# Five load semaphores instead of eight in a row-maximum kernel that streams its input

## The chip, the cores and the metric

One core of one Trainium2 chip. The metric is the device time of one execution in microseconds (us), median of several runs, lower is better. "Span" is the length of the profiled execution on the core; the timed number is some 1.8 us longer.

## The reference

```python
# x: 8192 x 8192 float32, standard normal
def reference(x):
    return np.linalg.norm(x, ord=np.inf, axis=1)   # the largest |x| of each row
```

Each element is read once, and almost nothing is written: 268.4 MB in, 32 KB out.

## The kernel before

A partition gets 64 rows: 47 "head" rows, in loads of two rows (one load has one row), and 17 "tail" rows, in 28 loads that shrink from 16384 columns to 704. SyncE issues all 52 loads, VectorE takes the maximum of the absolute values of each, GpSimd joins the parts of tail rows that were cut. Loads go to a ring of three places of 16384 columns. Load i counts on semaphore i modulo `SEMS`, and since a semaphore may count one load at a time, load i is issued only after the reduction of load i - `SEMS`. The ring adds a wait of its own: the reduction that last read the place must be done.

```python
P = 128
R = 2
RING = 3 * 16384
APART = 2048
SEMS = 8
# ... (sizes of the tail's loads)

class Pieces:
    def __init__(self, tc, ring):
        self.tc, self.nc, self.ring, self.head = tc, tc.nc, ring, 0
        self.sems = [tc.alloc_semaphore(f"loaded{i}") for i in range(SEMS)]
        # ...
    def load(self, at, w, src):
        i = self.started
        self.started += 1
        ins = self.nc.sync.dma_start(out=self.ring[:, at : at + w], in_=src)
        ins.then_inc(self.sems[i % SEMS], 16)
        # ...
        if i >= SEMS:
            self.tc.add_manual_dep(
                ins.ins,
                self.last[i - SEMS].name,
                # ...
                reason="the semaphore counts one load at a time",
            )
    def reduce(self, pairs):
        i = self.reduced
        self.reduced += 1
        for k, (dst, src) in enumerate(pairs):
            ins = self.nc.vector.tensor_reduce(
                out=dst, in_=src,
                axis=mybir.AxisListType.X, op=mybir.AluOpType.max,
                apply_absolute_value=True,
            )
            if k:
                self.tc.keep_in_program_order(ins)
            else:
                ins.wait_op(self.sems[i % SEMS], 16 * (i // SEMS + 1), "sem-ge")
            # ...
        self.last.append(ins.ins)
        return ins

# the head
    while row < head:
        n = (head - row) % R or R
        at = pieces.room(n * n_cols)
        pieces.load(at, n * n_cols, x_head[:, row * n_cols : (row + n) * n_cols])
        buf = ring[:, at : at + n * n_cols]
        pieces.reduce([(res_head[:, row : row + n], buf.rearrange("p (r m) -> p r m", r=n))])
        row += n
# ... (the tail, joining of parts, three stores)
```

## Time and profile before

| | before |
|---|---|
| time, median of 3 runs | 628.93 us (628.88 to 629.33) |
| span | 627.3 us |
| VectorE busy | 552.2 us, 88% |
| read from memory | 268.44 MB, 428 GB/s over the span |
| VectorE's wait for loads in the head | 70.5 us, 2.1 us a load once under way |
| last load issued, landed | 615.13, 624.0 |

To read it: the loads are one stream that SyncE keeps fed, so its end is set by bytes and rate as long as the queue of issued loads never runs dry. What can be lost is the *lead* of a load: the time from its issue to the landing of the load before it, which is how long the queue still has work. The prediction shows the lines.

### The profile page before, as it was taken

The page shows a single profiled execution, that of the slowest core. Times are in us where ns is not written, and L with a number is a line of the kernel's source. Part 1 is how long each engine was busy: PE and PEld are TensorE (multiplying, and loading weights), DVE is VectorE, ACT ScalarE, POOL GpSimd, SP SyncE. Part 2 cuts the span into 40 slices and gives each one's busy share as a digit, 9 for nine tenths or more (in the row PEclk, how much of TensorE's full clock was granted, in tenths as well). Part 3 has the DMA queues.
Part 4 walks back from the last instruction along what each step waited for, and adds up shares of the span by engine and source line. Part 5 has one row for each costly group of instructions (what it writes and reads, how often), then busy time and mean ns, then how long its engine had stood idle before and what let it go on. Part 6 is the DMA issues. An engine that isn't in the chain of part 4 may idle for free.

```text
span 627.3 us, 175 instructions
## 1 busy us (share of the span) xinstructions
DVE 552.2 (88%) x62; POOL 3.2 (1%) x14
## 2 busy tenths in 40 slices
DVE  1398888988889888898888998888988999999998
POOL 0000000000000000000000000000000000000000
DMA  9999999999999999999999999999999999999997
GB/s 401 401 468 401 468 401 468 401 468 401 468 401 468 401 468 401 460 410 451 418 443 426 443 426 439 430 422 447 405 464 406 454 410 442 430 422 429 425 423 306
DMA packets 7921, 268.48 MB, mean 428 GB/s; under 512 B 1264, under 2 KB 1264, under 8 KB 2416
## 3 DMA queue, kind: packets, MB, share of 16 engines
q1 hardware_dynamic: 7632, 268.44, 99.3%
q10 hardware_dynamic: 288, 0.03, 0.0%
q14 instruction: 1, 0.01, 0.0%
HBM read 268.44 MB, written 0.03 MB: 428 GB/s over the span
## 4 chain that ended last, share of the span: by engine, by line
DMA 58%; DVE 41%; issue 0%; DVEq 0%; SPq 0%
DMA ring<-in_x_dram 58%; DVE res_head L110 22%; DVE parts L110 12%; DVE res_tail L110 5%; DVE ring L110 1%; DVEq L269 0%; SPq L92 0%; DVE idle L222 0%
## 5 line engine op out<-in xcount | busy, mean ns | idle before, releaser
L110 DVE TENSOR_REDUCE res_head<-ring 128x2 f32<-128x16384 f32 (+1 forms) x24 | 404.8, 16865 | 70.5 <-DMA ring<-in_x_dram 70.5
L110 DVE TENSOR_REDUCE parts<-ring 128x1 f32<-128x3136 f32 (+18 forms) x22 | 78.5, 3633 | 0.1
L110 DVE TENSOR_REDUCE res_tail<-ring 128x1 f32<-128x8192 f32 (+1 forms) x8 | 61.2, 7703 | 2.1 <-DMA ring<-in_x_dram 2.1
L110 DVE TENSOR_REDUCE ring<-ring 128x1 f32<-128x1536 f32 (+4 forms) x6 | 8.2, 1443 | 0.0
L211 POOL TENSOR_SCALAR res_tail<-parts 128x1 f32<-128x1 f32 x9 | 2.7, 296 | 615.7 <-DVE parts L110 615.7
L211 POOL TENSOR_SCALAR parts<-parts 128x1 f32<-128x1 f32 x1 | 0.4, 354 | 5.6 <-DVE parts L110 5.6
L258 POOL MEMSET const-bfloat16-1.0<- 128x1 bf16 x1 | 0.1, 101 | 0.0
L258 POOL MEMSET const-uint8-127<- 128x1 uint8 x1 | 0.1, 101 | 0.0
L258 POOL MEMSET const-float32-0.0<- 128x1 f32 x1 | 0.1, 98 | 0.2 <-issue 0.2
L258 POOL MEMSET const-float32-1.0<- 128x1 f32 x1 | 0.1, 98 | 0.0
L222 DVE MEMSET idle<- 1x1 f32 x2 | 0.1, 59 | 0.0
## 6 DMA issues: line engine op xcount, KB each, us to landing
ring<-in_x_dram SPq DMA_DIRECT2D x3, 4096.0 KB, 39.7
ring<-in_x_dram SPq DMA_DIRECT2D x1, 6720.0 KB, 31.1
ring<-in_x_dram SPq DMA_DIRECT2D x1, 5568.0 KB, 34.6
ring<-in_x_dram SPq DMA_DIRECT2D x1, 4544.0 KB, 25.9
ring<-in_x_dram SPq DMA_DIRECT2D x1, 4224.0 KB, 29.5
ring<-in_x_dram SPq DMA_DIRECT2D x1, 4032.0 KB, 26.9
ring<-in_x_dram SPq DMA_DIRECT2D x1, 3584.0 KB, 35.1
ring<-in_x_dram SPq DMA_DIRECT2D x2, 1568.0 KB, 39.0
```

Of the source, the lines that this page charges most:

```text
L110: ins = self.nc.vector.tensor_reduce(out=dst, in_=src, axis=mybir.AxisListType.X, op=mybir.AluOpType.max, apply_absolute_value=True,)
L211: combined = nc.gpsimd.tensor_scalar(out=to, in0=best, scalar1=two[0], scalar2=two[1] if len(two) == 2 else None, op0=mybir.AluOpType.max, ...
L222: tc.keep_in_program_order(nc.vector.memset(idle[:, i : i + 1], 0.0))
L258: nc = _bacc.Bacc("TRN2", target_bir_lowering=False, num_devices=1)
```

## The change

Its intent is to use fewer semaphores, on the view that three spare ones do no work.

```diff
@@ -9,7 +9,7 @@
 R = 2
 RING = 3 * 16384
 APART = 2048
-SEMS = 8
+SEMS = 5
```

The one constant does two things: it sets how many semaphores there are, and how many loads may stand between issue and reduced.

## The prediction

> **What bounds the kernel now.** I read the page first, then the chain of waits in order of time, then the table of windows for the end, then the groups by form, the timeline of the last 70 us and the issues of transfers.
>
> The page, for the whole run:
>
> ```profile
> span 627.3 us, 175 instructions
> DVE 552.2 (88%) x62; POOL 3.2 (1%) x14
> DMA  9999999999999999999999999999999999999997
> HBM read 268.44 MB, written 0.03 MB: 428 GB/s over the span
> DMA 58%; DVE 41%; issue 0%; DVEq 0%; SPq 0%
> L110 DVE TENSOR_REDUCE res_head<-ring 128x2 f32<-128x16384 f32 (+1 forms) x24 | 404.8, 16865 | 70.5 <-DMA ring<-in_x_dram 70.5
> ```
>
> The input is 268.44 MB and it arrives at 428 GB/s over the span, with the transfer engines busy in every slice but the last. VectorE works 88% of the time and its only idle time to speak of, 70.5 us, is spent waiting for a load. The stream of loads is the bound. The table of windows says how it ends (columns: stretch, its length, VectorE busy, GpSimd busy, clock, share of the DMA engines, GB/s):
>
> ```profile
> 52.00:477.00 425.00, 378.47 (x22) 0.00 (x0) 1.00 1.00 433
> 545.00:600.00 55.00, 55.00 (x14) 1.67 (x6) 1.00 0.99 424
> 610.00:615.00 5.00, 5.00 (x3) 0.35 (x1) 1.00 1.01 419
> 620.00:624.00 4.00, 4.00 (x4) 0.00 (x0) 1.00 0.83 324
> ```
>
> In the head (47 rows a partition, loads of two rows) the loads set the pace at 433 GB/s and VectorE waits 2.1 us for each. In the tail (17 rows, 28 loads that shrink from 16384 to 704 columns) both are full: the loads are cut so that each lands just as VectorE has finished the one before. So there is no slack behind a late load in the tail: a landing that slips by 1 us moves the end by about 1 us. What has slack is the queue of loads ahead of VectorE. That is what the change touches, so I looked at who holds back the issuing of loads:
>
> ```profile
> SPq L92 <- DVE res_head L110: 465.4, 24, 27.5
> SPq L92 <- DVE parts L110: 90.9, 16, 20.0
> SPq L92 <- DVE res_tail L110: 40.0, 4, 13.9
> ```
>
> SyncE, which issues all loads, waits for a reduction before 44 of the 52. In the head this is for a place in the ring. In the tail the issues and the reductions stand like this (timeline, merged from several short windows; then the issues with KB and us to landing):
>
> ```profile
> 605.10 0.33 SPq L92 DMA_DIRECT2D ring<-in_x_dram  x1
> 613.07 0.33 SPq L92 DMA_DIRECT2D ring<-in_x_dram  x1
> 615.13 0.33 SPq L92 DMA_DIRECT2D ring<-in_x_dram  x1
> 618.35 2.80 DVE L110 TENSOR_REDUCE ring<-ring 128x1 f32<-128x1344 f32 x2
> 622.20 1.07 DVE L110 TENSOR_REDUCE ring<-ring 128x1 f32<-128x896 f32 x1
> ```
>
> ```profile
> ring<-in_x_dram SPq DMA_DIRECT2D x1, 384.0 KB, 10.1
> ring<-in_x_dram SPq DMA_DIRECT2D x1, 352.0 KB, 8.9
> ```
>
> The last load (352 KB) is issued at 615.13, at once after the 1920-column reduction that is eight loads before it, and lands 8.9 us later, at 624.0; VectorE reduces it from 624.05. The load before it lands at 613.07 + 10.1 = 623.2. So the last load spends nearly all of its 8.9 us standing in the queue behind others; its own bytes take the 0.8 us between these two landings.
>
> **What the Trainium skill says.** "DMA: Bandwidth & Descriptors", section "Why a DMA increments its semaphore by 16 and not by 1", asks for one semaphore for each load in flight, since two loads on one count can pass the wait early. The kernel keeps to that: load i waits until the reduction of load i - SEMS is done. So the number of semaphores is the number of loads that may stand between issue and reduced. The same page, section "Anatomy of one DMA", says that the wait is on the issuing sequencer and that the transfer engines only consume their queues; the trace agrees: the 44 waits before loads are SyncE's, and the DMA share stays near 1.0 through them. It gives about 2 us as the fixed part of a transfer, for another issuing path. Here the first load, into an empty queue, is issued at 0.72 and its reduction starts at 12.93: 12.2 us for 4.19 MB, which at 433 GB/s are 9.7 us. The fixed part is thus about 2.5 us in this trace, and I use that. "Latency and other measured facts" on that page has about 0.6 us to the first byte; here the DMA share is 0 up to 1.5 us and not up to 2.0, so 0.8 to 1.3 us after the issue.
>
> **The change part by part.** Nothing is added to the work: the same 52 loads of the same sizes at the same places, the same reductions, the same stores. Three semaphores go. The only thing that moves is when SyncE may issue a load: after the reduction of load i - 5 rather than i - 8, or after the last reader of its place in the ring, whichever is later.
>
> Head, loads 0 to 23: the ring has three places of two rows, so load i waits for reduction i - 3. Both 5 and 8 are weaker than that. Change: 0.
>
> Early tail, loads 24 to 33: working through the places that the code hands out, each overlaps a load at most five before it, so the ring still decides. Change: 0.
>
> Loads 34 to 51: here the ring would let nearly all of them go six or more loads behind, so with 8 semaphores the count decides from load 39 on, and with 5 from load 34 on. I put the issue right after the end of reduction i - 5 in the trace of before and compare with the landing of load i - 1, that is, how long the queue still has work. Load 37 moves most, from 546.9 to 572.5, and still has 16.8 us of queued work ahead of it. The lead shrinks with the loads: about 9 us at load 42, 5.2 at load 47, 4.6 at 48, 4.2 at 49, 3.7 at 50. For load 51 the releasing reduction is the 1344-column one: 618.35 + 1.54 (by form) = 619.89, so it issues at 619.9 rather than 615.1; the queue has work until 623.2, a lead of 3.2 to 3.3 us.
>
> A load is late only if the lead is shorter than the fixed 2.5 us. Load 51 from an empty queue would land at 619.93 + 2.5 + 0.83 = 623.3, but its turn in the queue comes at 624.0 anyway: 0.7 us to spare. Load 50: issued 618.5, 618.5 + 2.5 + 0.98 = 621.9 against 623.2: 1.2 us to spare. Load 49: 616.8 + 2.5 + 1.06 = 620.4 against 622.1: 1.8 us. All earlier ones have more. So every later issue is hidden, and the sum is 0 + 0 + 0 = 0 us. Three semaphores less may save some hundredths of a microsecond in setting up and clearing; no line of the page shows that cost, and I count 0.
>
> **The rivals.** First, *the queue runs dry at the end*: the 2.5 us was measured on a quiet chip start with one load of 4 MB, and a load issued into a busy queue might need more. At 4 us, load 51 would be late by 0.8 us and load 50 by 0.3; at 5 us the last four loads would be late by at most 1.8 us. These add up little, since a late reduction delays only the load five further on. Time 629.7 to 631. For it: the lead of 3.2 us is of the same size as the fixed part. Against it: what is needed early is the start of the transfer, 0.8 to 1.3 us after the issue, and the completion count overlaps with the next load.
>
> Second, *a shallower queue moves fewer bytes a second*: the sixteen engines of a load finish about 0.4 us apart in the trace, so an engine that runs ahead could be without work if only three loads stand behind the one being reduced. If loads 34 to 51 (some 46 us of transfer, 578 to 624) lost 1%, that is 0.5 us; 3% would be 1.4 us. Against it: at a lead of 3.2 us or more a spread of 0.4 us doesn't empty any queue, and the slowest engine sets the landing.
>
> Third, *a gain*: fewer queued loads disturb each other less, or the end of the program clears fewer semaphores. "Runtime: NRT & Kernel Launch", section on the launch sequence, has the reset of a fixed number of semaphores for each engine, so a smaller count would not shorten it; no run here shows it. The queue is served in order and the head, with only three loads at most outstanding, runs at 433 GB/s against 424 in the middle of the tail with more outstanding. But the tail's loads are smaller, which explains that by itself: each load costs a fixed bit more. At most -0.5 us, 628.4.
>
> **Range and chances.** The centre is the time before with no change, 628.93; I say 629.0, since the only sizeable risks lie above. Three runs of before spread over 0.45 us. The low end is that spread with a small gain, 628.4; the high end is the first rival at its mild form, one microsecond, 630.0. To leave the band of 2% the kernel would have to gain or lose 12.6 us. Nothing found can gain that, and a loss would need some 0.7 us at each of the 18 loads concerned. Chances: 0.01 faster, 0.98 same, 0.01 slower.
>
> **What would show each step right or wrong.** In the changed kernel the head must be the same to the hundredth (VectorE waiting 2.1 us for each load). SyncE's last load should be issued at about 619.9, with the time to landing of the 352 KB load down from 8.9 to about 4.1 us, the 384 KB load's from 10.1 to about 4.7, and landings at the same moments; VectorE should have no new idle time after 520 us, and the DMA share from 600 to 620 should stay at about 1.0. The first rival shows as idle time of VectorE before the 768- and 704-column pieces; the second as a lower rate from 578 us on and landings that slip gradually from load 34; the third as an earlier last landing or a shorter end after the last store. I would be wrong altogether if the head's loads came to wait for the count and not the ring.

## The result, and the profile after

| | before | after |
|---|---|---|
| time, median of 6 runs each | 628.99 us (628.88 to 629.33) | 628.97 us (628.86 to 629.36) |
| ratio | | 1.0, interval 0.9987 to 1.0012 |
| span | 627.3 us | 627.3 us |

The ratios and their 95% intervals come from runs of both kernels in the same rounds, so a ratio is not quite that of the medians. The page of the changed kernel:

```profile
span 627.3 us, 175 instructions
DVE 552.2 (88%) x62; POOL 3.2 (1%) x14
L110 DVE TENSOR_REDUCE res_head<-ring 128x2 f32<-128x16384 f32 (+1 forms) x24 | 404.8, 16865 | 70.5 <-DMA ring<-in_x_dram 70.5
```

The same span, the same instructions, the same 70.5 us of waiting in the head. What SyncE waited for, in the changed kernel (total us, times, longest):

```profile
SPq L92 <- DVE res_head L110: 465.3, 24, 27.5
SPq L92 <- DVE parts L110: 92.0, 16, 20.0
SPq L92 <- DVE res_tail L110: 40.0, 4, 13.9
SPq L92 <- DVE ring L110: 3.8, 3, 1.3
```

The first three are as before. The fourth is new: the last three loads now wait for reductions that write their parts into the ring, the ones five back. SyncE waits longer for its turn there, and no other engine pays for it. The timeline of the changed kernel (start, length), then its issues with KB and us to landing:

```profile
572.42 0.33 SPq L92 DMA_DIRECT2D ring<-in_x_dram  x1
619.90 0.33 SPq L92 DMA_DIRECT2D ring<-in_x_dram  x1
624.03 0.88 DVE L110 TENSOR_REDUCE res_tail<-ring 128x1 f32<-128x710 f32 x1
```

```profile
ring<-in_x_dram SPq DMA_DIRECT2D x1, 384.0 KB, 4.7
ring<-in_x_dram SPq DMA_DIRECT2D x1, 352.0 KB, 4.1
```

The last load is issued at 619.90, which is 4.8 us later than before (615.13), and is reduced from 624.03, where before it was 624.05. Its time to landing falls from 8.9 to 4.1 us: it only stands in the queue for a shorter time. Load 37, issued at 572.42 rather than 546.9, was moved most and also landed where it did before. The table of windows of the changed kernel (columns as in the prediction) for head and tail:

```profile
52.00:477.00 425.00, 378.48 (x22) 0.00 (x0) 1.00 1.00 433
520.00:624.00 104.00, 104.00 (x30) 2.38 (x8) 1.00 1.00 423
```

The rates are those of before (433 and, in the second window, also 423 GB/s), and VectorE has no idle time in the tail's last 104 us.

### The profile page after: what moved, and what is told of

It reads as the page before. It is cut to its first block, busy times and chain, and to the rows that moved or that the text cites. A ratio compares the mean times of both kernels' runs of the same rounds, so it can differ in the third digit from the quotient of the medians.

```text
span 627.3 us, 175 instructions
## 1 busy us (share of the span) xinstructions
DVE 552.2 (88%) x62; POOL 3.2 (1%) x14
## 4 chain that ended last, share of the span: by engine, by line
DMA 58%; DVE 41%; issue 0%; DVEq 0%; SPq 0%
DMA ring<-in_x_dram 58%; DVE res_head L110 22%; DVE parts L110 12%; DVE res_tail L110 5%; DVE ring L110 1%; DVEq L269 0%; SPq L92 0%; DVE idle L222 0%
## 5 line engine op out<-in xcount | busy, mean ns | idle before, releaser
L110 DVE TENSOR_REDUCE res_head<-ring 128x2 f32<-128x16384 f32 (+1 forms) x24 | 404.8, 16865 | 70.5 <-DMA ring<-in_x_dram 70.5
```

Of the source, the lines that this page charges most:

```text
L110: ins = self.nc.vector.tensor_reduce(out=dst, in_=src, axis=mybir.AxisListType.X, op=mybir.AluOpType.max, apply_absolute_value=True,)
```

## The experiments

The theory of the prediction (called A below): a load is late only if its lead is shorter than a fixed part of about 2.5 us, and with five semaphores the shortest lead is 3.2 us. Rivals: B, only the 1 us from issue to first packet counts; C, a loaded queue needs 4 us; D, a shallower queue lowers the rate. If A is right, fewer semaphores must begin to cost at a known point. Four kernels were written for that. Each edit is against the changed kernel.

### Four and three semaphores

```diff
-SEMS = 5
+SEMS = 4      # and, in a second kernel, 3
```

> Four semaphores, nothing else changed. Theory A (the five semaphores are free because a load needs about 2.5 us of queue ahead of it, the fixed part measured on the first load, and with five it has 3.2 us or more): the lead of the last load falls to about 1.95 us, below 2.5, so the end slips by 0.5 us, no load before load 49 is late; time about 629.5. Theory B (only about 1 us, issue to first packet, has to be covered): no change, 0.0 us. Theory C (a loaded queue needs some 4 us): 2.7 us longer, 631.7. Theory D (fewer loads in flight lower the rate of transfers): loads 32 to 45 already land later, with leads of 4 us and more.

> Three semaphores. A (2.5 us needed): head unchanged, since its ring has three places anyway; from about load 43 on the leads fall under 2.5 us, and lateness begins to feed itself, since a late reduction delays the issue three loads on: 3.5 us longer in all, about 632.4; 2.0 us needed would give 2.0 us, 3.0 us would give 5.0. B (1 us): 0.1 us. C (4 us): 9.3 us. D: landings slip in loads 27 to 38 already, where the leads are still 4 to 11 us.

Measured: with four 629.79 us against 628.84 (ratio 1.0015, interval 1.0002 to 1.0027); with three 634.71 against 628.84 (1.0093, 1.0079 to 1.0107). The timeline of the kernel with four:

```profile
624.00 0.95 DVE L110 TENSOR_REDUCE parts<-ring 128x1 f32<-128x768 f32 x1 [0.80 <-DMA ring<-in_x_dram]
624.92 0.89 DVE L110 TENSOR_REDUCE res_tail<-ring 128x1 f32<-128x710 f32 x1
```

VectorE's waits for loads in the tail, in the kernel with three (total us, times, longest):

```profile
DVE res_tail L110 <- DMA ring<-in_x_dram: 3.1, 2, 2.1
DVE parts L110 <- DMA ring<-in_x_dram: 2.0, 3, 0.9
DVE ring L110 <- DMA ring<-in_x_dram: 1.8, 3, 0.8
```

With four, one new gap of 0.8 us stands before load 50, whose lead was 2.2 us; load 49 with 2.6 us and all before it were in time. With three, VectorE waits in the tail at seven more places (2.1 us of the first line was there before), from load 42 on, where the lead is 2.8 us. Loads 27 to 41, with leads of 3.1 us and more, land at their usual intervals. So short leads begin to cost near the 2.5 us that A said; B (no change with four) falls, and D in its general form falls, since a halved queue with leads over 3 us moved the tail's bytes just as fast. But both losses are larger than A's (0.95 instead of 0.5, 5.9 instead of 3.5 us; C's 2.7 and 9.3 are too large), and one fixed threshold doesn't fit: with three, load 42 was 0.6 us late with a lead of 2.8 us, and load 43 another 0.9 us with 3.1 us, where loads 40 and 41 with the same 3.1 us had been in time.

### The last load alone

One load with a short lead, and none after it that could suffer.

```diff
-        if i >= SEMS:
+        back = 3 if i == 51 else SEMS      # and, in a second kernel, 4
+        if i >= back:
             self.tc.add_manual_dep(
                 ins.ins,
-                self.last[i - SEMS].name,
+                self.last[i - back].name,
```

> Five semaphores, but the last load alone waits for the reduction three before it, not five: issued at about 622.3 and not 619.9, so with a lead of 0.8 us. Nothing can feed back, as no load follows. A (2.5 us): lands at 622.3 + 2.5 + 0.83 = 625.6 rather than 624.0, 1.6 us longer. B (1 us): 0.1 us longer. C (4 us): 3.1 us longer. All other loads land as with five.

> Five semaphores, the last load alone waits for the reduction four before it: issued at about 621.2, lead about 1.95 us (0.78 us and 1.54 us late in last_three). A (F = 2.4): 621.2 + 2.4 + 0.83 = 624.4, 0.4 us late. N: its engines run dry about 1 to 1.4 us after the issue, so some start late: 1 to 2 us late, as much as or more than in last_three, though it is issued 1.1 us earlier.

(Theory N in the second text was formed between the two, from the next run but one.) Measured: waiting for the reduction three back 630.38 against 628.84 us (1.0024, interval 1.001 to 1.0038), four back 629.14 against 628.85 (1.0004, 0.999 to 1.0017). Timeline and issue of the kernel with three back:

```profile
622.28 0.33 SPq L92 DMA_DIRECT2D ring<-in_x_dram  x1
625.53 0.89 DVE L111 TENSOR_REDUCE res_tail<-ring 128x1 f32<-128x710 f32 x1 [1.42 <-DMA ring<-in_x_dram]
```

```profile
ring<-in_x_dram SPq DMA_DIRECT2D x1, 352.0 KB, 3.2
```

Its lead was 0.8 us, and 3.2 us from issue to landing less 0.83 us for its 352 KB at 433 GB/s leave a fixed part of 2.4 us. That is A's term, now measured where it is used, and the 1.5 us that it cost is A's 1.6. With four back (lead 1.9 us) the load took 3.0 us, so a fixed part of at most 2.2 us. In the trace it landed at 624.05, 0.1 us later than with five; the 0.3 us between the medians lie within the interval. That is a miss for N, which said 1 to 2, and less than A's 0.4: the fixed part is not quite the same for every load.

### Two semaphores, and the head alone

> Two semaphores: only one load can stand behind the one being reduced, in the head too. A (2.5 us needed): in the head the lead is about 2.1 us, so each two loads slip by about 0.4 us, some 5 us over 24 loads; in the tail each load waits out most of its fixed part: in all about 47 us longer, 676 (36 at 2.0 us, 59 at 3.0). B (1 us): 23 us longer and the head unchanged. C (4 us): 83 us longer. So this run measures the fixed part: the head's landings say it without the tail.

Edit: `SEMS = 2`. Measured: 696.64 us against 628.84 (1.1081, 1.1063 to 1.1099), so 68 us where A said 47 and C 83. The head, which A had slip 5 us, slipped 21 (its last load landed at 479.43 and not at 458.07), and 24 with the load after it. Some of its loads landed in A's time after their issue, others 2 us and more later: for load 3 the trace has all sixteen completion counts within 0.5 us, for load 5 eight of them in a group and eight some 1 to 2 us behind. So it is single transfer engines that come late. Theory N was put up for that: an engine that runs dry *shortly after* a new load is issued may start it later than one that was dry already. If so, issuing a load later can make it land no later. Three kernels test this, with the head alone at two back and the tail as with five. In the second and third, a small extra reduction delays each issue, and fits in VectorE's idle time (the declaration of its target `spare` is left out here).

```diff
+        back = 2 if i < 24 else SEMS
# in the delayed kernels also (448, and 960):
-        pieces.reduce([(res_head[:, row : row + n], buf.rearrange("p (r m) -> p r m", r=n))])
+        pieces.reduce([(res_head[:, row : row + n], buf.rearrange("p (r m) -> p r m", r=n)), (spare, buf[:, :960])])
```

> Five semaphores, but in the head (loads 0 to 23) each load waits for the reduction two before it; the tail is as with five. Each load then has a lead of about 2.1 us. Theory A (a load needs a fixed part F, 2.2 to 2.5 us, whatever the state of the queue): slip of (F - 2.07)/2 for each of 22 loads, 2 to 5 us in all: 631 to 634. Theory N (formed after the run with two semaphores: an engine whose queue runs dry about 1.0 to 1.5 us after the issue starts the new load only some 3 to 3.5 us after the issue, later than an engine that was dry before): about 24 us, as the head of that run had: about 653.

> As head_two, with a reduction of 448 columns into a spare column after each reduction of the head, which the load two further on waits for as well: each issue comes 0.5 us later, lead about 1.6 us. The result is unchanged, the extra reductions fit in VectorE's idle time. A: later is worse, (F + 0.5 - 2.07)/2 a load: 7 to 10 us over the time before, 636 to 639, about 5 us slower than head_two. N: less harm than head_two or about the same, 636 to 653, since the engines now run dry 0.5 to 1.0 us after the issue; which of the two is not known beforehand.

> As head_two_late_half, with 960 columns: issues 1.06 us later, lead about 1.0 us. A: (F + 1.06 - 2.07)/2 a load: 13 to 16 us over the time before, 642 to 645, some 11 us slower than head_two. N: the engines are dry by the time that the new load reaches them, so all start cleanly about 1 us after the issue: the same 13 to 16 us over the time before, but that is about 10 us FASTER than head_two, although every load is issued 1 us later.

| kernel | lead in the head, at first | time | runs from to | ratio to before (interval) |
|---|---|---|---|---|
| head_two | 2.1 us | 652.38 us | 651.27 to 654.26 | 1.0368 (1.0352 to 1.0384) |
| head_two_late_half | 1.5 us | 655.27 us | 653.35 to 657.97 | 1.0423 (1.0399 to 1.0447) |
| head_two_late | 1.0 us | 644.95 us | 644.49 to 645.11 | 1.0255 (1.0239 to 1.027) |

Loads 5 and 7 in the chain of waits of head_two, the kernel that isn't delayed (issue, length of the stretch from issue to landing):

```profile
88.45 23.87 DMA ring<-in_x_dram
129.59 21.76 DMA ring<-in_x_dram
```

and the same two loads in head_two_late, delayed by 1.06 us:

```profile
90.87 21.72 DMA ring<-in_x_dram
130.92 21.83 DMA ring<-in_x_dram
```

Load 5 was issued at 88.45 in one and at 90.87 in the other, and landed at 112.32 and 112.59: an issue 2.4 us later cost 0.3 us. In the delayed kernel loads take 2.2 to 2.6 us beyond their own 19.4 us at nearly every step, which is A's fixed part, and the total of 16 us is at the upper edge of what A and N both gave for it. In the undelayed one they take from 2.4 to 5.8 us; for every second load part of that is the wait behind a late one. So A fails on head_two (631 to 634 expected, 652 measured), and N's surprising claim, that all loads issued 1 us later would make the kernel faster, holds: 7.4 us faster, where N had said about 10. The half delay was no remedy: its 655 us lie above both ranges, A's 636 to 639 and N's 636 to 653.

The DMA packets of load 5 in the two traces show N's step itself. In head_two the engines ended the load before between 1.3 and 1.7 us after the issue of load 5. Six packets then followed without a gap; the first packets of the other ten engines started only 2.7 to 3.2 us after the issue, and took 2.6 to 3.3 us where the usual packet takes 2.4. In head_two_late the engines were dry 0.2 to 0.7 us after the issue, and all sixteen started 1.0 to 1.7 us after it, with first packets as slow. (They run dry some 0.4 us before the count that the lead is measured to.) The lead by itself doesn't decide, though: in the delayed kernel every second load had a lead of 2.4 us and none was late, and last_four had escaped at 1.9.

### How much lead is enough

To issue earlier than in head_two, each head reduction was cut in two, and the load two further on waits for the first part alone; its place in the ring was free a reduction earlier. The second part goes to a spare column, so the result is wrong for some rows (with 256 and 512 columns the comparison with the reference passed all the same, with 1536 it did not).

```diff
+        back = 2 if i < 24 else SEMS
-        self.last.append(ins.ins)
+        self.last.append(first if i < 24 else ins.ins)      # first: the first part
-        pieces.reduce([(res_head[:, row : row + n], buf.rearrange("p (r m) -> p r m", r=n))])
+        rows = buf.rearrange("p (r m) -> p r m", r=n)
+        cut = n_cols - 256      # 512, 1536
+        pieces.reduce([(res_head[:, row : row + n], rows[:, :, :cut]), (spare[:, :n], rows[:, :, cut:])])
```

> As head_two, but each head reduction is cut in two: first all but 256 columns of each row, then these 256 into a spare column; the load two further on waits for the first part alone (its place in the ring was free one reduction before). The result leaves out the maxima of those columns on purpose and is wrong for some rows. Issues come about 0.6 us earlier than in head_two, lead about 2.6 to 2.7 us. A (F = 2.4): no slip, the time before. N (an engine that runs dry somewhat after a new load was issued restarts late): the engines now run dry 1.6 to 2.0 us after the issue; if the new descriptors are safely there by then, the time before; if the danger reaches so far, up to 24 us longer. So this and the next run show how much lead is enough.

> As head_two_early with 512 columns in the second part: issues about 1.15 us earlier than in head_two, lead about 3.2 us, the lead that the last load has with five semaphores. A: the time before. N: at this lead the last load of the changed kernel was in time, so the time before or within 2 us of it; a slip of several us would say that the changed kernel's last loads are near the edge.

> As head_two_early with 1536 columns in the second part: the lead in the head is about 5.3 us. At leads of 2.6 and 3.2 us the stream still lost 15.6 and 13.6 us, with single transfer engines up to 2.5 us behind the others, and an engine that leads the last one by 2.5 us has that much less queue. If that is the cause, 5.3 us are enough even for the engine furthest ahead (5.3 - 2.5 = 2.8 against 1 us from issue to first packet, or 2.5 to landing): the time before within 1 us. If merely having one load queued behind another costs something, whatever the lead, it stays about 10 us longer. The result leaves out maxima on purpose, as in head_two_early.

| kernel | lead in the head, at first | time | runs from to | ratio to before (interval) |
|---|---|---|---|---|
| head_two_early | 2.6 us | 644.61 us | 642.44 to 647.33 | 1.0249 (1.0213 to 1.0285) |
| head_two_earlier | 3.2 us | 642.62 us | 639.11 to 645.14 | 1.0229 (1.0202 to 1.0256) |
| head_two_5us | 5.3 us | 629.57 us | 629.48 to 629.85 | 1.0011 (0.9994 to 1.0027) |

The windows of head_two, then of the kernel with 5.3 us, from 52 to 452 us (the last column is the rate):

```profile
52.00:452.00 400.00, 337.69 (x20) 0.00 (x0) 1.00 0.97 409
```

```profile
52.00:452.00 400.00, 358.56 (x41) 0.00 (x0) 1.00 1.00 433
```

A's "the time before" fails at 2.6 and 3.2 us. In both traces the first loads at two back are in time or nearly so, their sixteen counts within 0.7 us; then at load 6 single engines are late, the counts of one load spread to 2.4 us and stay spread by 1 to 3.4 us. With such a spread the engine that is ahead has that much less queue than the lead says, so it can run dry next; this last step is argued, not shown. At 5.3 us the rate is the full 433 GB/s, and only load 23, the last of the head, was 1 us late. The trace puts this 1 us in the middle of that load, on one engine, and so not down to the lead: a packet at 443.25, after a gap of 0.3 us, took 3.08 us instead of 2.42, just after an 8 KB packet of the instruction queue at 442.93. In the changed kernel this instruction packet comes at 624.5, after the last load. All five kernels with extra reductions have it in the head (442.9 to 472.4), with a slow packet of a load (2.95 to 3.08 us) 0.3 us behind it. So the added instructions probably have a cost of their own, of up to 1 us; no run separates it. The rest agrees with the expectation of a 2.5 us spread on top of 2.5 us, and speaks against a cost of merely having one load queued behind another.

### Count or depth

```diff
-SEMS = 5
+SEMS = 40
+DEPTH = 5
-        if i >= SEMS:
+        if i >= DEPTH:
-                self.last[i - SEMS].name,
+                self.last[i - DEPTH].name,
```

> Forty semaphores, of which no load shares one with any of the 39 before it, and still at most five loads between issue and reduced. If only the depth counts (the theory): the same as with five, issue of the last load at about 619.9, within 0.1 us of the time before. If the number of semaphores costs something in setting up, clearing or waiting (a rival of the prediction): 32 more than before, so any cost of some hundredths each would show as 1 us or more; the three fewer of the change would then have gained a tenth of that and hidden a loss of the same size.

Measured: 629.26 us against 628.92 (1.0006, 0.9992 to 1.002). The last load was issued at 619.86 and landed within 0.03 us of the kernel with five, so the depth alone sets when loads go. The five runs (629.10 to 629.48) nevertheless lie just above the nine of before (628.74 to 629.09). One place is seen: the instruction that clears semaphores at the end of the program took 0.29 us with forty, 0.11 with eight and 0.09 with five. That is 0.2 us of the 0.3; where the rest goes is open. Three fewer save 0.02 us, far below the spread.

## Why the prediction was right

*The head does not change.* Right: 70.5 us of waiting and 433 GB/s in both, since the ring, three places deep, is the stronger wait.

*The ring decides up to load 33, the count from 34 on.* Right: load 33 was issued at its old time, load 34 was the first to move (by 8.5 us), load 37 moved most.

*The last load is issued at 619.9, takes 4.1 us, lands when it did; the 384 KB load takes 4.7.* Right to 0.1 us, and so was "no new idle time", with a DMA share of 1.01 from 600 to 620 us.

*The fixed part of 2.5 us.* Right in size for a load that finds the queue all but dry: 2.4 us (last_three), at most 2.2 (last_four), 2.2 to 2.6 (head_two_late).

*"0.7 us to spare" and "a load is late only if the lead is shorter than the fixed 2.5 us".* This step carried the right conclusion, but it is not a safe margin, and that it held for the last loads is in part luck: with three semaphores load 43 was late with a lead of 3.1 us. In the head with two loads outstanding, leads of 2.6 and 3.2 us were not enough, since single engines came late by up to 2.5 us. In this the prediction's first rival ("a load issued into a busy queue might need more", 4 us) was nearer, and so was the second (an engine that runs ahead is left without work), which the prediction dismissed since the spread was 0.4 us: the spread stays at 0.4 us only as long as no engine has been late. That five semaphores are free rests on what was measured, six runs within 0.5 us and every load in time in the one that was traced, and not on the 0.7 us.

*Fewer semaphores to clear count 0.* 0.02 us in the trace. The remark that the count would not matter at the end was wrong for the kernel's own clearing, at that size.

Slips in the working, none of which changes a conclusion: 618.5 + 2.5 + 0.98 is 622.0 and not 621.9, and 384 KB take 0.91 us at 433 GB/s and not 0.98; with five semaphores four loads, not three, stand behind the one being reduced; the transfers of loads 34 to 51 run from 571.5, so they are 52.5 us and not 46. That a small load costs "a fixed bit more" is so in the trace of before: load 47 landed 1.43 us after load 46, and its 576 KB at 433 GB/s are 1.36 us.

Open: what makes one of sixteen engines start a queued load up to 2 us late, and why a lead of 2.4 us is enough in one kernel and 3.2 us not in another. The traces show the engine's gap and a slow first packet, and not the reason. Nor do the runs say how often the changed kernel's last loads, with leads of 3.2 to 4.3 us, would be hit over many more executions.

## What to carry to other kernels

A limit on the number of loads in flight costs nothing while the queue's lead, the time from a load's issue to the landing of the load before it, stays long; so work the lead out for every load, above all where loads get small, and compare it with issue-to-landing less the load's own bytes. Do not take the time that a lone load needs (2.4 us here) as the limit: in a running stream of 8 MB loads 3.2 us were too little and 5.3 us enough. And test a depth a step or two below the one that you want to ship: five cost nothing here, four 0.95 us, three 5.9, two 68.

## What the Trainium skill lacked or had wrong

- "DMA: Bandwidth & Descriptors", sections on queues and on the anatomy of one DMA: nothing on transfer engines that come late to a load which was queued before they ran dry. Here single engines lost up to 2 us or more each time, which took the head from 433 to 409 GB/s at a lead of 2.1 us, and issuing 1.06 us later made the kernel 7.4 us faster. Nor does that page have how much lead a stream needs: between 3.2 and 5.3 us in this head.
- The same page gives the fixed part as about 2.0 us, fitted on the path through GpSimd. On SyncE's path it was 2.4 us with the queue all but dry (3.2 us for 352 KB, last_three).
- The same page has about 0.6 us to the first byte on SyncE's path and doesn't say from when. Here it holds from the end of the issue: the first packet of the program started 0.63 us after that, and 1.0 us after the issue's start; in last_three and head_two_late engines that were dry before started 0.95 us after the start at the earliest.
- "Runtime: NRT & Kernel Launch", launch sequence: it has the reset around the kernel and not the clearing inside it, which grew with the count: 0.09 us for five semaphores of loads, 0.11 for eight, 0.29 for forty.
